# Column convolution of a convolution and recurrence block: two blocks of 256 tokens in one instruction

## The chip, the cores and the metric

The kernel runs on one core of one Trainium2 chip. The metric is device time in microseconds for one execution. The engines are TensorE (PE; its weight loads are PEld), VectorE (DVE), ScalarE (ACT), GpSimd (POOL) and the queue of SyncE (SP), which issues transfers.

## The reference

One layer over 4096 latent tokens of 1024 channels, a grid of 64 by 64. One projection of the normalised input gives q, two forget gates, v and a gate for a bidirectional gated recurrence (4 heads of 128), and u with two gates for a convolution of width 31: half of its 512 channels along the rows of the grid, half along its columns. Both branches are normalised, gated, put side by side, projected, added to the input and normalised again.

```python
def conformer_conv_latent(u, rows, conv_w_l, conv_b_l, ln_g_l, ln_b_l):
    grid = u.reshape(bsz, rows, GRID_W, ch)
    k_row = conv_w_l[:, :half].reshape(1, CONV_WIDTH, 1, half)
    k_col = conv_w_l[:, half:].reshape(CONV_WIDTH, 1, 1, half)
    y = jnp.concatenate([depthwise_conv2d(grid[..., :half], k_row),
                         depthwise_conv2d(grid[..., half:], k_col)], axis=-1).reshape(bsz, t, ch)
    return conv_tail(y, conv_b_l, ln_g_l, ln_b_l)      # silu(layernorm(y + conv_b))

def merge_branches(o_hgrn, g_a, conv_y, g_b, hgrn_norm_g_l, w_out_l):
    branch_a = head_rmsnorm(o_hgrn, hgrn_norm_g_l) * jax.nn.silu(g_a)
    branch_b = conv_y * jax.nn.silu(g_b)
    return jnp.concatenate([branch_a, branch_b], axis=-1) @ w_out_l

...
a_lat = rmsnorm(h_lat, norm_g[l]) * (1.0 + sc_l) + sh_l
q_l, zf_l, zb_l, v_l, ga_l, u_l, ug_l, gb_l = jnp.split(a_lat @ w_in[l], SPLITS, axis=-1)
o_l, _, _ = hgrn2_bidir(q_l, v_l, zf_l, zb_l, lb_f, lb_b, s_f, s_b)
y_l = conformer_conv_latent(u_l * jax.nn.sigmoid(ug_l), rows, conv_w[l], ...)
h_lat = h_lat + gt_l * merge_branches(o_l, ga_l, y_l, gb_l, hgrn_norm_g[l], w_out[l])
return rmsnorm(h_lat, final_norm_g)
```

The columns' convolution reads, for each token, the tokens 15 grid rows above it to 15 below, 960 tokens either way.

## The kernel before

Tokens are worked on in 16 blocks b of 256 (TB), and in 32 groups g of 128, two to a block. A **first sweep** goes through the blocks upward: projections, the recurrence hgrn(b) forward (with sums for the backward one kept for later), and the convolution along rows (`row_conv`, VectorE, L711), whose result goes to memory (`yrd`) for all blocks but the last. Block 15's stays in a tile `yc15`. A block's keys for the recurrence are split by ScalarE (L560) and VectorE (L561, `K`), turned by a transfer that SP issues (L562), and used by TensorE (`pu`, L578); `po` (L822, L823) is the recurrence's output, taken up into `op` (L828), `qu` (L837) is the last block's copy of a sum.

While the last blocks run, the gated inputs of the columns' convolution of all blocks come back from memory into one tile `gu_all` (L1001, 15 transfers on SP).

The **second sweep** goes through the groups downward, 31 to 0, since it needs the backward state `s_b`. Its parts are Python generators, which `merge` interleaves by their counts of steps:

- `gates(b)`: 48 matmuls of 512 columns (`ps_ga`, L1071) and 96 of 256 (`ps_gb`, L1083) for a block, each taken up by ScalarE (L1075, L1092). It is the work with which TensorE can fill time.
- `col_conv(b)`: VectorE alone. Two instructions for the middle tap (L1105), then 60 for the others (L1116), each over one half of the channels on 128 partitions and the 256 tokens of the block, fewer where the grid's edge cuts them.
- `group_front(g)`: `pi` (TensorE, L1144), `op` (VectorE adds, L1145), `s_b` (L1147), four transposes `ps_c` of the convolution's result (L1152), `bn_stats` (L1155) and what follows it, the seed of a reciprocal root (VectorE, L78), its three rounds of four small POOL instructions (L87 to L90), and ScalarE's `yn` (L1171) and `ops` (L1173).
- `group_back(g)`: four transposes `ps_d` of `yn` (L1188), silu, the gates, the split into two halves `yh`, `yl`, and the transposes `ps_o` (L1203).
- `group_out(g)`: 48 matmuls `py` (L1220), the residual `xr` (L1224), a last norm with POOL's L84 and L85, and the transfer out (L1235).

In one turn of the loop at L1252, `group_out(g)`, `group_back(g - 1)`, `group_front(g - 2)`, half of a convolution and half of a block's gates are merged; the convolution of a block runs some two groups ahead of its use. Tiles come from pools: `e1` holds named places ("A", "xt", "gu0" to "gu2") for both sweeps, `m1` only for the first, `m2` only for the second, so a tile in `m2` must wait until the first sweep has let `m1` go. A scheduler then sets one fixed order for each engine; every engine works through its own in order, and stands still where the next instruction's input is not there.

Of the kernel before, what the change touches and what calls it, by code (L numbers as in the profile page):

```python
# [98 lines left out]
def hymba_block(  # L99
# [97 lines left out]
    with ExitStack() as s1:  # L197
# [855 lines left out]
    with ExitStack() as s2:  # L1053
# [8 lines left out]
        def gates(b, d):  # L1062
# [14 lines left out]
            for ct in (0, 2):  # L1077
# [169 lines left out]
        fng = e1.tile([P, D], F32, tag="A", name="fng")  # L1247
        fg1 = final_norm_g.rearrange("(o n) -> o n", o=1)
        nc.sync.dma_start(fng, bass.AP(fg1.tensor, fg1.offset, [[0, P], [1, D]]))

        gate = conv = None
        for g in range(NG + 1, -1, -1):  # L1252
            gens = []
            if g < NG:
                gens.append((N_OUT, group_out(g, ds[g // 2])))
            if 0 < g <= NG:
                gens.append((N_BACK, group_back(g - 1, ds[(g - 1) // 2])))
            if g > 1:
                if g > 2:
                    load_group2(g - 3, ds[(g - 3) // 2])  # L1260
                gens.append((N_FRONT, group_front(g - 2, ds[(g - 2) // 2])))
            b = g // 2 - 2
            if g % 2:
                if 0 <= b:
                    conv = col_conv(b, ds[b])
                    gens.append((31, part(conv, 31)))
                if gate:
                    gens.append((7, gate))
                    gate = None
            else:  # L1270
                if conv:
                    gens.append((31, conv))
                    conv = None
                if 0 < b < NB - 2:
                    load_block(b - 1, ds[b - 1])
                if 0 <= b < NB - 2:
                    gate = gates(b, ds[b])
                    gens.append((7, part(gate, 7)))
                elif gate:
                    gens.append((7, gate))  # L1280
                    gate = None
            if g == NG + 1:
                gate = gates(NB - 2, ds[NB - 2])
                gens.append((7, part(gate, 7)))
# [29 lines left out]
```

## Time and profile before

| | |
|---|---|
| median of 3 runs | 2177.08 us (2176.64 to 2177.74) |
| the profiled execution | 2179.47 us, of which the span is 2177.7 us |
| busy share of the span | PE 94%, PEld 70%, DVE 81%, ACT 46%, POOL 17% |
| instructions | PE 22339, DVE 4283, ACT 2326, POOL 886 |
| the column convolution's taps, L1116 | 828 into `ycs`, 345.3 us, 471 ns each in the mean |

The profiled execution is read as one timeline. Busy time is the time in which an engine has work in it; where VectorE's instructions follow one another without a gap, their times overlap a little, so the distance from start to start is what one costs. A number in brackets behind a row of the timeline is the idle time ahead of it and what ended it. "issue" is time for which no releaser is seen.

### The profile page before, as it was taken

The numbers are of one execution on the slowest core, as the hardware profiler recorded it, in microseconds if no ns is written. First come the engines' busy times: TensorE is split into PE (matmuls) and PEld (weight loads), VectorE is DVE, ScalarE is ACT, GpSimd is POOL, SyncE is SP. The second block draws the span as 40 slices with busy tenths as digits, with TensorE's granted clock in tenths as the row PEclk, the third lists the DMA queues.
The fourth block names the chain that finished last, engine by engine and source line by source line (L and its number), as shares of the span: only waits on it lengthen the run. The fifth ranks groups of instructions, "written<-read, shape, count | busy, mean of one in ns | idle before, by whom it ended". The sixth has DMA issues, their size and how long they took to land. (4 is left out here: it accounts for less than half of the span.)

```text
span 2177.7 us, 54464 instructions
## 1 busy us (share of the span) xinstructions
PE 2056.2 (94%) x22339; PEld 1517.2 (70%) x22339; DVE 1757.6 (81%) x4283; ACT 1006.0 (46%) x2326; POOL 371.6 (17%) x886
## 2 busy tenths in 40 slices
PE   6999999999998998999999999989999999999998
PEld 3777778778777887777788888655555555565664
DVE  5988877977975978978887975969999888888744
ACT  4944546445446445455445434433343333343343
POOL 1110101101101101101101100013433333333222
PEclk8999999999999999999999999989999999999999
DMA  9436155335235254253333225443332222333221
GB/s 363 136 90 161 60 151 161 69 113 130 71 113 144 74 145 138 63 161 114 74 108 63 52 55 156 152 155 102 107 107 93 97 98 92 120 120 115 97 78 59
DMA packets 222082, 247.96 MB, mean 114 GB/s; under 512 B 143652, under 2 KB 151672, under 8 KB 217864
## 3 DMA queue, kind: packets, MB, share of 16 engines
q1 hardware_dynamic: 221288, 240.19, 37.8%
q8 instruction: 175, 2.87, 0.6%
q0 software_dynamic: 544, 4.29, 0.5%
q14 instruction: 75, 0.61, 0.1%
HBM read 138.52 MB, written 72.36 MB: 97 GB/s over the span
## 5 line engine op out<-in xcount | busy, mean ns | idle before, releaser
L289 PEld LDWEIGHTS <-w 128*128 128x128 f16 x4704 | 456.2, 98 | 61.8 <-issue 3.6
L711 DVE SCALAR_TENSOR_TENSOR yr<-gu,convw,yr 128x224 f32<-128x224 f32 (+2 forms) x900 | 357.9, 445 | 0.0
L1116 DVE SCALAR_TENSOR_TENSOR ycs<-gu_all,convw,ycs 128x256 f32<-128x256 f32 (+2 forms) x828 | 345.3, 471 | 0.0
L289 PEld LDWEIGHTS <-pair 128*128 128x128 f16 x3168 | 308.2, 98 | 39.4 <-issue 0.6
L1220 PE MATMUL py<-wo,yh 128*128 128x512 f16 x1024 | 251.4, 381 | 2.9 <-ACT yh L1204 2.9
L289 PE MATMUL ps_z<-aT,pair 128*128 128x256 f16 x1632 | 190.8, 276 | 0.0
L289 PE MATMUL ps_z<-aT,w 128*128 128x256 f16 x1632 | 188.6, 274 | 1.9 <-DVE aT L247 1.4
L1083 PE MATMUL ps_gb<-aT,w 128*128 128x256 f16 x1536 | 187.7, 273 | 0.0
L81 POOL TENSOR_SCALAR xqh<-xssq 128x1 f32<-128x1 f32 x30 | 12.5, 416 | 1022.8 <-DVE xssq L262 1022.8
L300 PE MATMUL pv<-w,aT 128*128 128x512 f16 x816 | 184.4, 379 | 1.3 <-DVE gu L675 1.3
L1071 PE MATMUL ps_ga<-w,aT 128*128 128x512 f16 x768 | 182.1, 382 | 0.0
L289 PE MATMUL ps_u<-aT,w 128*128 128x256 f16 x1536 | 181.3, 274 | 0.2 <-ACT q L657 0.2
L756 ACT COPY km<-X 128x512 f32<-128x512 f32 x160 | 107.9, 675 | 156.1 <-DVE X L764 155.8
L289 PE MATMUL ps_g<-aT,w 128*128 128x256 f16 x1536 | 177.8, 273 | 0.6 <-ACT q L657 0.6
L1220 PEld LDWEIGHTS <-yh 128*128 128x128 f16 x1024 | 100.4, 98 | 108.5 <-ACT yh L1204 4.0
L289 PE MATMUL ps_q<-aT,pair 128*128 128x256 f16 x1536 | 173.3, 273 | 0.0
L1083 PEld LDWEIGHTS <-w 128*128 128x128 f16 x1536 | 150.1, 98 | 31.8
L300 PEld LDWEIGHTS <-aT 128*128 128x128 f16 x816 | 77.4, 98 | 88.2 <-issue 1.5
L1071 PEld LDWEIGHTS <-aT 128*128 128x128 f16 x768 | 75.5, 99 | 81.6 <-issue 2.5
L1220 PE MATMUL py<-wo,yl 128*128 128x512 f16 x512 | 129.6, 379 | 0.0
L1226 ACT ACTIVATE jk<-xr 128x512 bf16<-128x512 f32 x64 | 40.3, 629 | 184.7 <-DVE xr L1224 128.4
L319 ACT ACTIVATE f<-f,lbv,oml 128x128 f32<-128x128 f32 x272 | 112.9, 486 | 0.0
(308 smaller groups left out, 3301.5 us busy)
## 6 DMA issues: line engine op xcount, KB each, us to landing
xt<-in_x_dram SPq DMA_DIRECT2D x32, 512.0 KB, 4.3
xr<-in_x_dram SPq DMA_DIRECT2D x32, 512.0 KB, 3.6
out_dram<-xr SPq DMA_DIRECT2D x31, 512.0 KB, 2.6
aTd<-aT SPq DMA_DIRECT2D x14, 1024.0 KB, 5.1
aT<-aTd SPq DMA_DIRECT2D x14, 1024.0 KB, 5.2
wst<-in_w_in_dram SPq DMA_DIRECT2D x16, 512.0 KB, 4.3
qb<-qbd SPq DMA_DIRECT2D x32, 256.0 KB, 2.7
ub<-ubd SPq DMA_DIRECT2D x32, 256.0 KB, 2.7
```

The costliest lines, as they stand in the source:

```text
L81: eng.tensor_scalar(h, v, -0.5, 0.0, ALU.mult, ALU.add)
L289: nc.tensor.matmul(ps[:, j, :], w[:, wi, k, (ct + j) * P : (ct + j + 1) * P], aT[:, ai, k, :], start=n == 0, stop=n == 23)
L300: nc.tensor.matmul(pv, aT[:, ai, k, i * P : (i + 1) * P], W[G_V][:, wi, k, :], start=n == 0, stop=n == 23)
L319: nc.scalar.activation(fa, fa, AF.Identity, scale=oml[:, d, ct + j : ct + j + 1], bias=lbv[:, d, ct + j : ct + j + 1])
L711: nc.vector.scalar_tensor_tensor(ar[i][:, :, lo:hi], gr[i][:, :, lo + dl : hi + dl], convw[:, i, j : j + 1], ar[i][:, :, lo:hi], ALU.mult, ...
L756: nc.scalar.copy(fap(km, 0, kd), fap(Xs[gi], 0, ks))
L1071: nc.tensor.matmul(ps, aT[:, ai, k, i * P : (i + 1) * P], Wa[:, wi, k, :], start=n == 0, stop=n == 23)
L1083: nc.tensor.matmul(ps[:, j, :], Wb[:, wi, k, (ct + j) * P : (ct + j + 1) * P], aT[:, ai, k, :], start=n == 0, stop=n == 23)
L1116: nc.vector.scalar_tensor_tensor(ya, gu_all[:, i, (lo + dl) * GW : (hi + dl) * GW], convw[:, 2 + i, j : j + 1], ya, ALU.mult, ALU.add)
L1220: nc.tensor.matmul(py, y[:, k // 4, k % 4, :], W2["o", nh][:, wi, k, :], start=n == 0, stop=n == 23)
L1226: nc.scalar.activation(junk, h[:, sl], AF.Square, accum_out=hs[:, nh : nh + 1])
```

## The change

The columns' convolution is done for two blocks at once (a pair p of blocks 2p and 2p + 1), over 512 tokens in one instruction, for pairs 6 to 0. The last two blocks, 15 and 14, which the second sweep needs first, are still done one by one, 256 tokens wide, but now both into one tile `ycl` in the place "A" of `e1`. Row results no longer share a tile with column results: block 15's lie in `yr15` (place "gu2"), those of the others are fetched by a new `load_rows` into `yrow`. So the gates of even blocks use the places "gu0" and "gu1" instead of "gu2" and "gu1". The last norm's factors `fng` move from "A" to "xt". In a turn of the loop 15 or 16 steps of a pair's convolution stand where 31 of a block's stood, over four turns instead of two; pair 6 begins in the first turn, beside block 14's 61 steps.

```diff
@@ row_conv @@
-                late["yc"] = e1.tile([P, 4, TB], F32, tag="A", name="yc15")
-            acc = late["yc"][:, 0:2, :] if b == NB - 1 else m1.tile([P, 2, TB], F32, tag="yr", name="yr")
+                late["yc"] = e1.tile([P, 2, TB], F32, tag="gu2", name="yr15")
+            acc = late["yc"] if b == NB - 1 else m1.tile([P, 2, TB], F32, tag="yr", name="yr")
@@ gates @@
-                    gb = e1.tile([P, 2, TB], F32, tag=f"gu{2 - ct // 2}", name="gb")
+                    gb = e1.tile([P, 2, TB], F32, tag=f"gu{ct // 2}", name="gb")
@@ col_conv @@
-        def col_conv(b, d):
-            yc = late["yc"] if b == NB - 1 else m2.tile([P, 4, TB], F32, tag="ycs", name="ycs", bufs=2)
-            d["yc"] = yc
+        def load_rows(b, d):
+            d["yr"] = late["yc"] if b == NB - 1 else m2.tile([P, 2, TB], F32, tag="yrow", name="yrow", bufs=2)
             if b < NB - 1:
-                nc.sync.dma_start(yc[:, 0:2, :], yrd[b])
-            r0 = b * TB // GW
-            nr = TB // GW
+                nc.sync.dma_start(d["yr"], yrd[b])
+
+        def col_conv(p, half=None):
+
+            if half is None:
+                yc = m2.tile([P, 2, 2 * TB], F32, tag="ycs", name="ycs", bufs=2)
+            elif half:
+                late["ycl"] = yc = e1.tile([P, 2, 2 * TB], F32, tag="A", name="ycl")
+            else:
+                yc = late["ycl"]
...
+            r0 = 2 * p * TB // GW
+            nr = 2 * TB // GW
+            if half is not None:
+                r0, nr = r0 + half * TB // GW, TB // GW
+                yc = ds[2 * p + half]["yc"]
...
@@ second sweep @@
-        merge((N_COL, col_conv(NB - 1, ds[NB - 1])), (N_GATE, gates(NB - 1, ds[NB - 1])))
+        merge((N_COL, col_conv(NB // 2 - 1, 1)), (N_GATE, gates(NB - 1, ds[NB - 1])))
...
+        gate = gates(NB - 2, ds[NB - 2])
+        first = col_conv(NB // 2 - 1, 0)
         for g in range(NG + 1, -1, -1):
...
+            if g >= NG:
+                gens += [(N_GATE // 2, part(gate, N_GATE // 2) if g > NG else gate), (31, part(first, 31 if g > NG else 30))]
+                if g == NG:
+                    gate = None
+            if g % 4 == 1 and g >= 9:
+                conv = col_conv((g - 9) // 4)
+            if conv:
+                n = 15 if (g - 9) % 4 != 2 else 16
+                gens.append((n, part(conv, n)))
+                if g % 4 == 2:
+                    conv = None
```

Line numbers shift: the taps L1116 become L1129, `op` L1145 becomes L1158, `bn_stats` L1155 becomes L1168, `ps_c` L1152 becomes L1165, `ps_d` L1188 becomes L1201.

**Order, first place.** VectorE at the end of the first sweep, from the last step of block 14's keys on (`K`, L561; `s_f`, L583, is the forward state, `FL` L539 belongs to block 15). Before:

```order
L774 TENSOR_TENSOR X_18578<-X_18578,FL_18580 128x8x64
L561 SCALAR_TENSOR_TENSOR K_19356<-X_18577,K_19356 128x512
L561 SCALAR_TENSOR_TENSOR K_19360<-X_18577,K_19360 128x512
L561 SCALAR_TENSOR_TENSOR K_19375<-X_18578,K_19375 128x512
L561 SCALAR_TENSOR_TENSOR K_19379<-X_18578,K_19379 128x512
L583 SCALAR_TENSOR_TENSOR s_f_270<-s_f_270,FL_18579,pu_19391 128x128 x4
L539 TENSOR_TENSOR FL_19493<-f_18739 128x2x256
```

After:

```order
L774 TENSOR_TENSOR X_18578<-X_18578,FL_18580 128x8x64
L1118 TENSOR_SCALAR ycl_20310<-gu_all_19490,convw_83,vec_82 128x256 x2
L561 SCALAR_TENSOR_TENSOR K_19356<-X_18577,K_19356 128x512
L561 SCALAR_TENSOR_TENSOR K_19360<-X_18577,K_19360 128x512
L1129 SCALAR_TENSOR_TENSOR ycl_20310<-gu_all_19490,convw_83,ycl_20310 128x256 x12
L561 SCALAR_TENSOR_TENSOR K_19375<-X_18578,K_19375 128x512
L1129 SCALAR_TENSOR_TENSOR ycl_20310<-gu_all_19490,convw_83,ycl_20310 128x256 x2
L561 SCALAR_TENSOR_TENSOR K_19379<-X_18578,K_19379 128x512
L1129 SCALAR_TENSOR_TENSOR ycl_20310<-gu_all_19490,convw_83,ycl_20310 128x256 x2
```

The taps of block 14 (`ycl`, `x12` for twelve in a row) now stand between the four `K`, where nothing stood.

**Order, second place.** ScalarE in hgrn of block 15 (`K` L560, `qu` and `ub` L837, `v16` L568, `op` L828, `gb` the gates' results). Before:

```order
L1075 ACTIVATE ga_20529<-ps_ga_20584,es_91 128x512
L560 ACTIVATE K_20174<-X_19492 128x512
L560 ACTIVATE K_20178<-X_19492 128x512
L837 ACTIVATE qu_20182<-pu_20191,es_91 128x512
L568 ACTIVATE v16_20209<-v_19893 128x512
L1092 ACTIVATE gb_20764<-ps_gb_20648,es_91 128x512
L828 ACTIVATE op_20243<-po_20230,es_91 128x512
L1092 ACTIVATE gb_20847<-ps_gb_20766,es_91 128x512
```

After:

```order
L560 ACTIVATE K_20174<-X_19492 128x512
L560 ACTIVATE K_20178<-X_19492 128x512
L1092 ACTIVATE gb_20882<-ps_gb_20793,es_91 128x512
L837 ACTIVATE qu_20182<-pu_20191,es_91 128x512
L568 ACTIVATE v16_20209<-v_19893 128x512
L1092 ACTIVATE gb_20791<-ps_gb_20664,es_91 128x512
L828 ACTIVATE op_20243<-po_20230,es_91 128x512
L837 ACTIVATE ub_20262<-pu_20249,es_91 128x512
```

One `gb` went ahead of `qu`, and the other, which lies in the place "gu0", stands ahead of `op` with nothing between.

**Order, third place.** VectorE around `bn_stats` of group 27, the first group of block 13 (`yn`, `ops`, `yl` are the groups' own steps, `xr` and `hv` those of the last norm). Before, with the taps into one tile:

```order
L1147 SCALAR_TENSOR_TENSOR s_b_84<-s_b_84,fb_all_85,ub_21041 128x128
L1116 SCALAR_TENSOR_TENSOR ycs_21321<-gu_all_19490,convw_83,ycs_21321 128x256
L1195 TENSOR_TENSOR yn_20999<-yn_20999,gb_20847 128x256
L1116 SCALAR_TENSOR_TENSOR ycs_21321<-gu_all_19490,convw_83,ycs_21321 128x256
L1192 TENSOR_TENSOR ops_20849<-ops_20849,ga_20529 128x512
L1155 BN_STATS bs_21373<-ps_c_21368 128x6
L1116 SCALAR_TENSOR_TENSOR ycs_21321<-gu_all_19490,convw_83,ycs_21321 128x256
L1205 SCALAR_TENSOR_TENSOR yl_21142<-ps_o_21214,ky_251,yh_21141 128x512
```

After, with the taps into two tiles, of pair 6 (`ycs_20540`) and of pair 5 (`ycs_21335`):

```order
L1129 SCALAR_TENSOR_TENSOR ycs_21335<-gu_all_19490,convw_83,ycs_21335 128x512
L1247 SCALAR_TENSOR_TENSOR xr_21072<-xr_21072,hr_21537,fng_20687 128x1024
L1129 SCALAR_TENSOR_TENSOR ycs_21335<-gu_all_19490,convw_83,ycs_21335 128x512
L1129 SCALAR_TENSOR_TENSOR ycs_20540<-gu_all_19490,convw_83,ycs_20540 128x448 x2
L1129 SCALAR_TENSOR_TENSOR ycs_21335<-gu_all_19490,convw_83,ycs_21335 128x512 x2
L1237 SCALAR_TENSOR_TENSOR xr_21313<-py_21679,kinv_254,xr_21313 128x512
L1129 SCALAR_TENSOR_TENSOR ycs_20540<-gu_all_19490,convw_83,ycs_20540 128x384 x2
L1129 SCALAR_TENSOR_TENSOR ycs_21335<-gu_all_19490,convw_83,ycs_21335 128x512 x2
L1168 BN_STATS bs_21382<-ps_c_21377 128x6
L1129 SCALAR_TENSOR_TENSOR ycs_20540<-gu_all_19490,convw_83,ycs_20540 128x320
```

Narrow taps at the edge of pair 6 and wide ones of pair 5 alternate ahead of `bn_stats`.

## Rows read from the trace of the kernel before

**Rows 1.** Table of stretches: start:end, length, then busy time of each engine, PEclk the granted clock.

```profile
core 0: us, PE busy (x) PEld busy (x) DVE busy (x) ACT busy (x) POOL busy (x), PEclk, DMA share, GB/s
1340.00:1420.00 80.00, 77.67 (x1005) 54.85 (x1003) 70.94 (x174) 30.63 (x58) 1.17 (x2) 1.00 0.60 178
1420.00:1440.00 20.00, 19.69 (x168) 14.79 (x167) 5.19 (x14) 4.77 (x8) 0.00 (x0) 1.00 0.32 93
1440.00:1460.00 20.00, 12.07 (x70) 8.69 (x68) 18.39 (x54) 8.42 (x28) 4.21 (x15) 0.73 0.82 289
1560.00:1860.00 300.00, 283.72 (x1694) 171.01 (x1692) 261.98 (x676) 107.64 (x305) 104.62 (x253) 0.99 0.32 106
1860.00:2170.00 310.00, 308.92 (x1846) 185.06 (x1846) 218.69 (x553) 121.73 (x339) 88.05 (x274) 1.00 0.28 94
```

**Rows 2.** TensorE's own timeline: start, length, engine, line, operation, shapes, count, idle before.

```profile
1380.37 1.89 PE L1071 MATMUL ps_ga<-w,aT 128*128 128x512 f16 x8
...
1544.38 0.66 PE L1188 MATMUL ps_d<-ident,yn 128*128 128x128 f32 x4 [1.21 <-ACT yn L1171]
...
1755.31 1.46 PE L1220 MATMUL py<-wo,yh 128*128 128x512 f16 x6
...
2167.32 1.89 PE L1220 MATMUL py<-wo,yl 128*128 128x512 f16 x8
```

**Rows 3.** TensorE's waits (total us, times, longest us): 1360 to 1560, then 1560 to 2178.

```profile
PE ps_d L1188 <- ACT yn L1171: 8.2, 3, 3.8
PE pi L1144 <- DMA qb<-qbd: 2.3, 1, 2.3
...
PE ps_d L1188 <- ACT yn L1171: 14.4, 7, 3.0
```

**Rows 4.** Timeline at group 21: TensorE, VectorE, POOL, ScalarE.

```profile
1741.85 0.60 PE L1152 MATMUL ps_c<-ident,ycs 128*128 128x128 f32 x4
...
1759.75 0.94 PE L1188 MATMUL ps_d<-ident,yn 128*128 128x128 f32 x4 [2.98 <-ACT yn L1171]
...
1747.23 0.69 DVE L1155 BATCH_NORM_STATS2 bs<-ps_c 128x6 f32<-128x512 f32 x1
...
1752.90 0.17 DVE L78 TENSOR_SCALAR or<-osq 128x5 int32<-128x5 int32 x1
1752.97 3.64 DVE L1116 SCALAR_TENSOR_TENSOR ycs<-gu_all,convw,ycs 128x256 f32<-128x256 f32 x9
1756.53 0.74 DVE L1205 SCALAR_TENSOR_TENSOR yl<-ps_o,ky,yh 128x512 f16<-128x512 f32 x1
1757.19 0.87 DVE L1116 SCALAR_TENSOR_TENSOR ycs<-gu_all,convw,ycs 128x256 f32<-128x256 f32 x2
...
1753.99 0.31 POOL L89 TENSOR_SCALAR ort<-ort 128x5 f32<-128x5 f32 x1
1754.38 0.31 POOL L90 TENSOR_TENSOR or<-or,ort 128x5 f32<-128x5 f32 x1
...
1757.03 0.20 POOL L89 TENSOR_SCALAR ort<-ort 128x5 f32<-128x5 f32 x1
1757.31 0.41 POOL L90 TENSOR_TENSOR or<-or,ort 128x5 f32<-128x5 f32 x1
...
1758.94 0.76 ACT L1171 ACTIVATE yn<-ps_c,lnm,or 128x512 f32<-128x512 f32 x1
```

**Rows 5.** Timeline at the first sweep's end: VectorE, then SP's queue.

```profile
1348.68 0.69 DVE L561 SCALAR_TENSOR_TENSOR K<-X,K 128x512 f16<-128x512 f32 x1 [7.63 <-ACT K L560]
...
1414.45 0.69 DVE L561 SCALAR_TENSOR_TENSOR K<-X,K 128x512 f16<-128x512 f32 x1
...
1443.10 0.68 DVE L1145 TENSOR_TENSOR op<-pi,op 128x512 f32<-128x512 f32 x1
...
1340.91 0.52 SPq L1001 DMA_DIRECT2D gu_all<-gud  x1
1341.54 5.24 SPq L562 DMA_TRANSPOSE X<-K  x2
```

More of the change, by code (lines that the diff above doesn't have):

```diff
@@ L1095, in hymba_block @@
         N_GATE = 14
-        def col_conv(b, d):
-            yc = late["yc"] if b == NB - 1 else m2.tile([P, 4, TB], F32, tag="ycs", name="ycs", bufs=2)
-            d["yc"] = yc
+        def load_rows(b, d):
+            d["yr"] = late["yc"] if b == NB - 1 else m2.tile([P, 2, TB], F32, tag="yrow", name="yrow", bufs=2)
             if b < NB - 1:
-                nc.sync.dma_start(yc[:, 0:2, :], yrd[b])
-            r0 = b * TB // GW
-            nr = TB // GW
+                nc.sync.dma_start(d["yr"], yrd[b])
[6 more added lines that the diff above has]
+                yc = late["ycl"]
+            for b in (2 * p, 2 * p + 1):
+                ds[b]["yc"] = yc[:, :, (b % 2) * TB : (b % 2 + 1) * TB]
+            r0 = 2 * p * TB // GW
[3 more added lines that the diff above has]
+                yc = ds[2 * p + half]["yc"]
             for i in range(2):
-                nc.vector.tensor_scalar(yc[:, 2 + i, :], gu_all[:, i, b * TB : (b + 1) * TB], convw[:, 2 + i, HALF : HALF + 1],
+                nc.vector.tensor_scalar(yc[:, i, :], gu_all[:, i, r0 * GW : (r0 + nr) * GW], convw[:, 2 + i, HALF : HALF + 1],
                                         vec[:, R_CB + 2 + i : R_CB + 3 + i], ALU.mult, ALU.add)
@@ L1114, in col_conv @@
                     if lo < hi:
-                        ya = yc[:, 2 + i, (lo - r0) * GW : (hi - r0) * GW]
+                        ya = yc[:, i, (lo - r0) * GW : (hi - r0) * GW]
                         nc.vector.scalar_tensor_tensor(ya, gu_all[:, i, (lo + dl) * GW : (hi + dl) * GW], convw[:, 2 + i, j : j + 1],
@@ L1138, in group_front @@
             op, ub, qb = d[g]
-            yc = d["yc"]
+            yr, yc = d["yr"], d["yc"]
             tk = slice(gi * P, (gi + 1) * P)
@@ L1151, in group_front @@
             for j in range(4):
-                nc.tensor.transpose(ps[:, j * P : (j + 1) * P], yc[:, j, tk], ident)
+                nc.tensor.transpose(ps[:, j * P : (j + 1) * P], (yr if j < 2 else yc)[:, j % 2, tk], ident)
             bs = sm.tile([P, 6], F32, tag="bs", name="bs")
@@ L1242, in hymba_block @@
             ds[b]["aT"] = aTs[b]
-        merge((N_COL, col_conv(NB - 1, ds[NB - 1])), (N_GATE, gates(NB - 1, ds[NB - 1])))
+        merge((N_COL, col_conv(NB // 2 - 1, 1)), (N_GATE, gates(NB - 1, ds[NB - 1])))
+        load_rows(NB - 1, ds[NB - 1])
+        load_rows(NB - 2, ds[NB - 2])
         for g in (NG - 1, NG - 2):
@@ L1246, in hymba_block @@
         load_block(NB - 3, ds[NB - 3])
[L1247 to L1251, printed above, removed]
+        conv = None
+        gate = gates(NB - 2, ds[NB - 2])
+        first = col_conv(NB // 2 - 1, 0)
         for g in range(NG + 1, -1, -1):
             gens = []
+            if g == NG:
+                fng = e1.tile([P, D], F32, tag="xt", name="fng", bufs=2)
+                fg1 = final_norm_g.rearrange("(o n) -> o n", o=1)
+                nc.sync.dma_start(fng, bass.AP(fg1.tensor, fg1.offset, [[0, P], [1, D]]))
             if g < NG:
@@ L1261, in hymba_block @@
                 gens.append((N_FRONT, group_front(g - 2, ds[(g - 2) // 2])))
+            if g >= NG:
+                gens += [(N_GATE // 2, part(gate, N_GATE // 2) if g > NG else gate), (31, part(first, 31 if g > NG else 30))]
+                if g == NG:
+                    gate = None
[5 more added lines that the diff above has]
+                if g % 4 == 2:
+                    conv = None
             b = g // 2 - 2
             if g % 2:
[L1264 to L1268, printed above, removed]
-                    gate = None
[L1270 to L1274, printed above, removed]
-                    load_block(b - 1, ds[b - 1])
[L1276 to L1284, printed above, removed]
+                if b >= 0:
+                    load_rows(b, ds[b])
+                if gate and g < NG:
+                    gens.append((N_GATE // 2, gate))
+                    gate = None
+            elif 0 <= b < NB - 2:
+                if b > 0:
+                    load_block(b - 1, ds[b - 1])
+                gate = gates(b, ds[b])
+                gens.append((N_GATE // 2, part(gate, N_GATE // 2)))
             merge(*gens)
```

## The prediction

> **What bounds the kernel now.** I read the page's shares and slices first, then a table of stretches, TensorE's waits, VectorE's groups, and last the engines side by side at one stall. The change acts only from the end of the first sweep on, some 840 us. From 1860 to 2170 us TensorE is busy 308.9 of 310 us; from 1560 to 1860 it is busy 283.7 of 300 us, and in 1440 to 1460 us only 12.1 of 20 us, at a granted clock of 0.73 [rows 1]. The reader is to see that only these holes can be won: the work itself, 743.4 us from the first gate matmul at 1380.37 us to the last `py`, is the same in both kernels, and the last `py` starts at about 2168.8 us [rows 2]. (The price of a 512-column matmul is 0.216 us, from six in 1.46 us and eight in 1.89 us [rows 2]; 256 columns are half.) So TensorE loses 2168.8 - 1380.4 - 743.4 = 45.0 us in all. At `ps_d` of group 26, at 1544.38 us, 140.6 us of work were done, so 23.4 us were lost by then: the **start-up part**. The other 21.6 us are lost until 1860 us: the **steady part**.
>
> Who makes the holes? TensorE's waits name `ps_d` behind `yn` first: 8.2 us of 1360 to 1560 us and 14.4 us behind that [rows 3]. ScalarE is not the cause, it is only last in a chain. At group 21 [rows 4] `ps_c` is done at 1742.45 us, but VectorE comes to `bn_stats` only at 1747.23 and to the seed L78 at 1752.90, since convolution taps stand ahead; then twelve small POOL steps, `yn` at 1758.94, and `ps_d` at 1759.75 after 2.98 us of standing still. From L78 to `ps_d` are 6.9 us. VectorE, busy 262.0 of 300 us there [rows 1], sets the steady holes through its queue.
>
> **The wide taps.** Nine taps over 256 columns take 3.64 us and two 0.87, so one follows the other after (3.64 - 0.87) / 7 = 0.396 us [rows 4]. No tap over 512 columns is in this trace; nearest is the same instruction over 512 columns with one input in PSUM, L1205, after which the next starts 0.66 us later [rows 4]. Bounds for a wide tap: 0.66 us, and 2 x 0.396 = 0.79 if width saved nothing. I take 0.66, the same form and size. The straight line through the two is 0.128 us and 1.04 ns a column. The sweep's convolution goes from 896 instructions to 502, 394 fewer, of which each saved 0.128 us: 49 us of VectorE time, about 7 us for each pair of blocks. Nothing of it is TensorE's; it counts only where a hole is.
>
> [...]
>
> **Steady part.** Before, the four groups of two blocks carry 45, 17, 45 and 17 taps of 0.396 us, after 29, 21, 12 and 0 of 0.66 us. Other work of VectorE is about 7.9 us a group, TensorE's is 23 us (both from their orders, each instruction at such a start-to-start price). Before, a heavy group needs 17.8 + 7.9 = 25.7 us against 23, and stalls about 3 us; those are the holes at groups 23, 21, 19, 17, 15 and 13. After, the heaviest needs 19.1 + 7.9 = 27.0 us, but the one ahead of it needs 7.9 and leaves VectorE waiting, and in TensorE's new order `ps_d` of every fourth group stands 3.3 us later. Bounds: 0 left of the 21.6 us, or all of it (nothing shows that only the average counts). I take 2 us left, since in the rows VectorE falls behind only where a heavy group follows one that used up its slack.
>
> **The end of the first sweep.** The changed kernel computes block 14's column taps there, 46 instructions, about 18 us with the two first, in VectorE's order between the `K` of blocks 14 and 15. Before, VectorE is busy 70.9 of 80 us there [rows 1]; one gap of 7.63 us stands ahead of `K` at 1348.68 us [rows 5]. Twelve taps fall into that gap, but they need transfers of `gu_all`, of which SP issues the sixth at 1340.91 us [rows 5], and two more of these issues now go ahead of the transposes on SP; so I let `K` start 2 to 3 us later, and the first `K` of block 15 (1414.45 us [rows 5]) about 7 us later. The chain from there to `op` of group 31 (1443.10 us [rows 5]) is hgrn(15)'s own: transposes, `pu`, `qu`, `v`, `po`. In it TensorE's order has less gate work as filler, and ScalarE's order now has `gb` in `gu0` ahead of `op`, where it must wait for the last row tap that reads `gu0`; together I put 3 us on these. `op` of group 31 comes at 1453, 10 us later; bounds +4 (if the gap takes most of the taps) and +14 (if all but 4 us of the 18 lie on the path).
>
> **Start-up of the second sweep.** Pair 6 must be done over its full width before group 27 is read, and VectorE's order mixes pair 5's taps in as well. Pricing each instruction in VectorE's order from `op` of group 31 on, L78 of groups 30, 27 and 26 comes after 15.2, 73.2 and 85.2 us before, and after 27.7, 107.6 and 112.6 us now. TensorE's work ahead of their `ps_d` is 74.9, 154.3 and 158.3 us now (140.6 for group 26 before). What TensorE must have lost by group 26, if VectorE never stands still, is 1453 + 112.6 + 6.9 - 1380.4 - 158.3 = 33.8 us. The same sum for before gives 1443.1 + 85.2 + 6.9 - 1380.4 - 140.6 = 14.2 against 23.4 measured, so VectorE's own waits (for ACT, POOL, `py`) add 9.2 us. I take 6 for after, since more taps stand ready as filler; bounds 3 and 10.
>
> **POOL beside wide taps.** In [rows 4] POOL's steps follow each other after 0.39 us while 256-column taps run, and after 0.28 us while L1205 runs, which reads one input from PSUM: a step gets through once per tap. If that holds, steps beside wide taps come every 0.66 us. [...] By [rows 4], the chain from L78 to the end of the last POOL step, 4.8 us before, takes up to 6.7 us where ten wide taps stand behind L78 (0.66 us for 0.40 in the steps beside them). At group 27 that adds 1.6 us, and its sum, 1453 + 107.6 + 6.9 - 1380.4 - 154.3 = 32.8 us, becomes 34.4; with 6 us of waits the start-up part is about 41 us where before it was 23.4: **17 us lost**.
>
> The sum: 41 + 2 = 43 us against 45, 2 us less. The tail after the last `py`, 8.9 us, has no convolution and stays. Other edits (row results in their own tiles, fetched as before; `fng` in another tile a little later) I cost at nothing: their transfers are issued groups ahead of their readers; without that cover the nearest row is the 2.3 us for which `pi` waits for `qb` [rows 3]. The profiled execution took 2179.47 us, 2.4 above the median of 2177.08; 2177.5 by its measure is **2175 us** as a median.
>
> **The rivals.** (a) *Forecast*: start-up loss and steady gain nearly cancel, 2170 to 2181, centre 2175. Chance 0.50. (b) *The start-up is hardly later*: block 14's taps fit into VectorE's gaps (5.2 of 20 us busy in 1420 to 1440 us [rows 1] speaks for room, though those gaps lie behind `K`). `op` +2 to +7 us and waits of 3 to 4 us make 29 to 36 us lost, with 2 steady 31 to 38: 2163 to 2170. Chance 0.28. (c) *Slower by the start-up*: `op` of group 31 +14 us and 10 us of waits, so 33.8 + 4 + 10 + 1.6 = 49.4, and 2 steady: 51 us, 2183. It decides from `op` later than about 1456 us. For it speaks that VectorE is nearly full from 1350 to 1418, against it the 15 us free behind. Chance 0.12. (d) *POOL takes VectorE's place*: the chain behind L78 grows by 2 us and the heavy group is 27.0 - 24.5 = 2.5 us above TensorE's work between the two `ps_d`; if the slack of the light group doesn't carry over, up to 4.5 us in each of some four groups, 18 us after 41: 59 us, 2191; at half of that 2182. Chance 0.07. (e) *Width saves nothing* (0.79 us a tap): pair 6's taps ahead of group 27 cost some 7 us more and the heavy groups 23 + 7.9 = 31 us: above 2185. Chance 0.03, since L1205's row speaks against it.
>
> **How the numbers follow.** A measurement here tells about 0.2%, 4.4 us, from no change: below 2172.7 is faster, above 2181.5 slower. (a) splits 0.10, 0.38, 0.02; (b) is all faster; (c) 0.02 same and 0.10 slower; (d) and (e) slower. Together 0.38 faster, 0.40 same, 0.22 slower. The range reaches to the ends of (b) and (c), with 2 us for their own terms above, and leaves out what lies beyond them of (b), (d) and (e): 2163 to 2185.
>
> **What would show it.** Right: conv taps over 512 columns starting 0.66 us apart; `op` of group 31 near 1453; `ps_d` of group 26 near 1380 + 158 + 41 = 1580 us; next to no wait of `ps_d` from 1620 us on; POOL's steps 0.66 us apart beside taps; the period of a block 46 us from then on. Wrong: `op` of group 31 before 1449 (then (b)), after 1456 (c), or waits of `ps_d` on `yn` above 6 us behind 1620 us (d).

## The result: 0.8% slower, and the profile after

The changed kernel takes 2193.8 us (median of 4 runs, 2192.36 to 2196.29) against 2176.87 us of the kernel before (4 runs): ratio 1.0078, 95% interval 1.0063 to 1.0093, some 17 us **slower**. The forecast was 2175, the range 2163 to 2185. The later comparisons ran on other chips, where the kernel before takes 2168.15, 2176.66 and 2176.08 us in the median and its single executions spread by 15 to 20 us; every ratio below stands against runs of the kernel before on the same chip.

The page of after, its first rows (busy time of each engine, share of the span, instructions):

```profile
span 2190.6 us, 54071 instructions
## 1 busy us (share of the span) xinstructions
PE 2062.7 (94%) x22339; PEld 1522.2 (69%) x22339; DVE 1709.8 (78%) x3889; ACT 1006.8 (46%) x2326; POOL 386.7 (18%) x886
```

VectorE is busy 1709.8 us instead of 1757.6: the work went down as planned. The span grew by 12.9 us all the same. The same table of stretches as [rows 1]:

```profile
core 0: us, PE busy (x) PEld busy (x) DVE busy (x) ACT busy (x) POOL busy (x), PEclk, DMA share, GB/s
1440.00:1460.00 20.00, 8.83 (x63) 6.62 (x61) 14.58 (x30) 4.72 (x17) 4.63 (x13) 0.77 0.63 224
1460.00:1480.00 20.00, 16.98 (x68) 9.24 (x68) 19.18 (x40) 6.53 (x22) 5.32 (x13) 0.72 0.24 79
1560.00:1860.00 300.00, 283.70 (x1682) 172.07 (x1681) 233.49 (x467) 117.65 (x335) 112.53 (x280) 0.98 0.30 103
1860.00:2170.00 310.00, 306.48 (x1842) 185.19 (x1841) 180.37 (x391) 121.30 (x336) 88.61 (x267) 0.99 0.29 96
```

From 1560 to 1860 us VectorE has 233.5 us of work where it had 262.0, and TensorE is still busy 283.7 us, as it was. From 1440 to 1480 us TensorE works 25.8 of 40 us, at a mean granted clock of 0.77 and 0.72 in the two halves. Before it worked 32.1 us there, at 0.73 [rows 1] and, in the second half, 0.92:

```profile
1460.00:1480.00 20.00, 20.00 (x115) 11.68 (x113) 18.81 (x46) 10.97 (x34) 3.66 (x12) 0.92 0.13 41
```

TensorE's waits (total, times, longest), first up to 1580 us, then behind it, to be set beside [rows 3]:

```profile
engine line waited for: us in total, times, longest us
PE ps_d L1201 <- ACT yn L1184: 10.5, 3, 4.3
PE pi L1157 <- DVE ycs L1129: 7.8, 1, 7.8
...
PE ps_d L1201 <- ACT yn L1184: 15.3, 8, 3.1
```

The eight stand at groups 23, 22, 19, 18, 15, 14, 11 and 7, the longest (2.9, 2.9 and 3.1 us) at 19, 15 and 11. Before, the seven of [rows 3] stood at groups 25, 22, 21, 19, 17, 15 and 13, so not quite where the prediction has them.

I call **lost** at a group the start of its first `ps_d`, less the first gate matmul, less the work in TensorE's order between them, as in the prediction. (A 256-column matmul costs 0.109 us, since in before eight of `ps_gb` take 1.04 us and sixteen 1.91.) For after, the first gate matmul starts at 1378.51 us, `ps_d` of group 26 at 1574.77 with 158.3 us of work ahead, `ps_d` of group 0 at 2165.83 with 727.2: lost are 38.0 us by group 26 and 60.1 us by group 0. Before it was 23.4 and 45.3. So the start-up part lost 14.6 us more, and the steady part is 22.1 us as against 21.9: **nothing of the steady part came back**. The first gate matmul came 1.9 us earlier, so the span grew by 14.8 - 1.9 = 12.9 us.

Group 15 of after, as [rows 4] shows one of before (TensorE, VectorE, POOL, ScalarE; `lnm` is POOL's last step ahead of `yn`):

```profile
1800.14 0.38 PE L1165 MATMUL ps_c<-ident,ycs 128*128 128x128 f32 x2
...
1820.98 0.66 PE L1201 MATMUL ps_d<-ident,yn 128*128 128x128 f32 x4 [2.87 <-ACT yn L1184]
...
1804.76 0.69 DVE L1168 BATCH_NORM_STATS2 bs<-ps_c 128x6 f32<-128x512 f32 x1
...
1812.03 0.17 DVE L78 TENSOR_SCALAR or<-osq 128x5 int32<-128x5 int32 x1
1812.11 1.41 DVE L1129 SCALAR_TENSOR_TENSOR ycs<-gu_all,convw,ycs 128x512 f32<-128x512 f32 x2
1813.43 0.74 DVE L1218 SCALAR_TENSOR_TENSOR yl<-ps_o,ky,yh 128x512 f16<-128x512 f32 x1
1814.09 3.39 DVE L1129 SCALAR_TENSOR_TENSOR ycs<-gu_all,convw,ycs 128x512 f32<-128x512 f32 x5
...
1813.66 0.20 POOL L89 TENSOR_SCALAR ort<-ort 128x5 f32<-128x5 f32 x1
1813.94 0.20 POOL L90 TENSOR_TENSOR or<-or,ort 128x5 f32<-128x5 f32 x1
...
1814.96 0.59 POOL L88 TENSOR_TENSOR ort<-ort,osq 128x5 f32<-128x5 f32 x1
1815.64 0.57 POOL L89 TENSOR_SCALAR ort<-ort 128x5 f32<-128x5 f32 x1
1816.30 0.58 POOL L90 TENSOR_TENSOR or<-or,ort 128x5 f32<-128x5 f32 x1
1816.95 0.58 POOL L87 TENSOR_TENSOR ort<-or 128x5 f32<-128x5 f32 x1
...
1818.49 0.26 POOL L1181 TENSOR_SCALAR lnm<-ba,or 128x1 f32<-128x1 f32 x1
...
1818.41 1.28 ACT L1186 ACTIVATE ops<-ops,or 128x128 f32<-128x128 f32 x4 [9.35 <-POOL or L90]
1819.60 0.67 ACT L1092 ACTIVATE gb<-ps_gb,es 128x512 f32<-128x512 f32 x1
1820.17 0.76 ACT L1184 ACTIVATE yn<-ps_c,lnm,or 128x512 f32<-128x512 f32 x1
```

Wide taps start 0.66 us apart ((3.39 - 1.41) / 3). Beside them POOL's steps start 0.68, 0.66 and 0.65 us apart; beside L1218, which reads PSUM, 0.28 us. TensorE stands still for 2.87 us at `ps_d`. The steps of the chain, from the end of `ps_c` on, in us (each the difference of two starts or ends in the timelines):

| group 15 | to `bn_stats` | to L78 | to the end of POOL's last step | to `yn` | to `ps_d` | sum | of it TensorE waits |
|---|---|---|---|---|---|---|---|
| before | 4.2 | 5.7 | 5.3 | 0.7 | 0.8 | 16.7 | 2.4 |
| after | 4.2 | 7.3 | 6.7 | 1.4 | 0.8 | 20.5 | 2.9 |
| halves (256 columns, below) | 2.2 | 8.0 | 5.3 | 0.8 | 2.1 | 18.3 | 0 |
| each tap twice (below) | 2.2 | 8.0 | 5.3 | 0.7 | 2.0 | 18.3 | 0 |
| two rounds (below) | 3.4 | 7.3 | 5.2 | 0.8 | 0.8 | 17.5 | 1.7 |
| every second tap (below) | 4.2 | 6.6 | 3.9 | 0.9 | 0.8 | 16.4 | 0.1 |
| after, taps held back (below) | 3.8 | 1.1 | 6.3 | 0.8 | 2.7 | 14.8 | 0 |

TensorE's order has 17.6 us of work between `ps_c` and `ps_d` here (20.5 - 2.9), and had 14.3 before. The new order does put `ps_d` 3.3 us later, as the prediction read; the chain grew by 3.7: 1.6 up to L78, 1.4 in POOL's steps, and 0.7 ahead of `yn`, since ScalarE's order now has a `gb` (L1092) between `ops` and `yn`, which stood behind `yn` before.

The wait is the idle time ahead of `ps_d` in TensorE's timeline. The sum less the wait is TensorE's work in between, and the order that is made anew for each kernel sets it too (15.8 us with two rounds, 18.3 in halves): each experiment shows its edit together with a new order. ([Rows 4] and the prediction call their group 21. Counted from the first `ps_d`, of group 31, it is group 17, with 4.8, 5.7, 5.3, 0.7 and 0.8 us; the reading does not hang on the number.)

### The profile page after: what moved, and what is told of

Its sections match the earlier page's. It is cut to its first block, busy times and chain, and to the rows that moved or that the text cites. A ratio compares the mean times of both kernels' runs of the same rounds, so it can differ in the third digit from the quotient of the medians.

```text
span 2190.6 us, 54071 instructions
## 1 busy us (share of the span) xinstructions
PE 2062.7 (94%) x22339; PEld 1522.2 (69%) x22339; DVE 1709.8 (78%) x3889; ACT 1006.8 (46%) x2326; POOL 386.7 (18%) x886
## 3 DMA queue, kind: packets, MB, share of 16 engines
q8 instruction: 175, 2.87, 0.6%
## 5 line engine op out<-in xcount | busy, mean ns | idle before, releaser
L711 DVE SCALAR_TENSOR_TENSOR yr<-gu,convw,yr 128x196 f32<-128x196 f32 (+14 forms) x960 | 382.5, 447 | 0.0
L1129 DVE SCALAR_TENSOR_TENSOR ycs<-gu_all,convw,ycs 128x512 f32<-128x512 f32 (+6 forms) x404 | 272.6, 716 | 0.0
L81 POOL TENSOR_SCALAR xqh<-xssq 128x1 f32<-128x1 f32 x30 | 12.1, 404 | 1023.3 <-DVE xssq L262 1023.3
```

Source lines behind the costliest of these rows:

```text
L81: eng.tensor_scalar(h, v, -0.5, 0.0, ALU.mult, ALU.add)
```

## Experiments

Lost time in all kernels, in us, with the starts from which it is worked out:

| kernel | first gate matmul | `ps_d` 26, work ahead | lost by 26 | `ps_d` 0, work ahead | lost by 0 | behind 26 | ratio to before (95%) |
|---|---|---|---|---|---|---|---|
| before | 1380.37 | 1544.38, 140.6 | 23.4 | 2152.85, 727.2 | 45.3 | 21.9 | 1 |
| after | 1378.51 | 1574.77, 158.3 | 38.0 | 2165.83, 727.2 | 60.1 | 22.1 | 1.0078 (1.0063 to 1.0093) |
| after, again | 1380.05 | 1575.93, 158.3 | 37.6 | 2171.02, 727.2 | 63.8 | 26.2 | 1.0077 (1.0049 to 1.0106) |
| halves | 1376.47 | 1579.90, 156.5 | 46.9 | 2153.55, 727.2 | 49.9 | 3.0 | 1.0043 (1.0028 to 1.0058) |
| each tap twice | 1377.53 | 1586.45, 163.0 | 45.9 | 2162.01, 727.2 | 57.3 | 11.4 | 1.0049 (1.0025 to 1.0074) |
| every second tap | 1379.74 | 1555.09, 143.3 | 32.0 | 2139.61, 727.2 | 32.7 | 0.7 | 0.9974 (0.9960 to 0.9988) |
| after, taps held back | 1373.48 | 1545.17, 139.9 | 31.7 | 2148.59, 727.2 | 47.9 | 16.2 | 1.0047 (1.0032 to 1.0062) |
| before, taps held back | 1374.43 | 1541.27, 142.0 | 24.8 | 2141.89, 727.2 | 40.3 | 15.5 | 1.0015 (1.0001 to 1.0030) |
| pair 6 in halves | 1376.65 | 1583.83, 164.3 | 42.9 | 2170.98, 727.2 | 67.1 | 24.2 | 1.0088 (1.0059 to 1.0117) |
| block by block in own tiles | 1377.68 | 1544.23, 137.0 | 29.6 | 2153.92, 727.2 | 49.0 | 19.4 | 0.9972 (0.9948 to 0.9996) |
| the same, again | 1375.17 | 1540.10, 137.0 | 28.0 | 2146.65, 727.2 | 44.3 | 16.3 | 1.0015 (0.9996 to 1.0034) |
| after, two rounds | 1377.31 | 1572.04, 158.6 | 36.1 | 2150.13, 726.1 | 46.7 | 10.6 | 1.0005 (0.9988 to 1.0022) |
| before, two rounds | 1381.34 | 1548.89, 143.2 | 24.4 | 2141.32, 726.1 | 33.9 | 9.5 | 0.9945 (0.9923 to 0.9967) |
| own tiles, two rounds | 1379.46 | 1542.54, 137.4 | 25.7 | 2135.16, 726.1 | 29.6 | 3.9 | 0.9937 (0.9916 to 0.9957) |

The work is rounded, so a difference can be off by 0.1. A lost time is one profiled execution; after and after again differ by 4 us behind group 26, so differences below 5 us there say nothing. The kernel before was profiled on the first chip alone. What a kernel costs is therefore read from the ratios, and the lost times only tell where it goes.

### What keeps the steady part

**Halves.**

```diff
...
+            elif True:
+                for h in (1, 0):
+                    yield from taps(ds[2 * p + h]["yc"], r0 + h * TB // GW, TB // GW)
...
-                n = 15 if (g - 9) % 4 != 2 else 16
+                n = 31 if (g - 9) % 4 > 1 else 30
```

Here `taps` is the loop over the taps of `col_conv`; `h` is 1 for the odd block, which is needed first.

> The changed kernel, but each pair's convolution in two halves of 256 columns, the odd block (needed first) ahead of the even one; everything else as changed. Two theories of why the steady part still loses 22 us (ps_d of group 26 to the end). Queue theory: taps stand in clumps ahead of a group's short chain on VectorE (48, 37, 26, 8 taps of 0.396 us in four groups here, 29, 21, 6, 4 of 0.66 us in the changed kernel), width does not matter: steady part 22 to 28 us, POOL's steps back to 0.39 us apart. POOL theory: the stalls remain because POOL's steps wait 0.66 us behind wide taps: steady part falls to about 10 us. Start-up part (36 us in the changed kernel): 31 to 36, since only the odd half must be done before group 27. Time: queue 2190 to 2200, POOL 2175 to 2182.

Measured 1.0043. Behind group 26 3.0 us are lost, not 22 to 28: the queue theory falls as I had put it, although the clumps are as long in time as those of after, and VectorE has 48 us more work. Group 15 of this kernel (VectorE, POOL, TensorE):

```profile
1811.16 0.16 DVE L78 TENSOR_SCALAR or<-osq 128x5 int32<-128x5 int32 x1
...
1812.69 3.64 DVE L1135 SCALAR_TENSOR_TENSOR ycs<-gu_all,convw,ycs 128x256 f32<-128x256 f32 x9
...
1814.87 0.32 POOL L88 TENSOR_TENSOR ort<-ort,osq 128x5 f32<-128x5 f32 x1
1815.28 0.31 POOL L89 TENSOR_SCALAR ort<-ort 128x5 f32<-128x5 f32 x1
1815.67 0.31 POOL L90 TENSOR_TENSOR or<-or,ort 128x5 f32<-128x5 f32 x1
...
1819.26 0.60 PE L1207 MATMUL ps_d<-ident,yn 128*128 128x128 f32 x4
```

POOL's steps stand 0.41 and 0.39 us apart again, and `ps_d` has no wait. Behind 1580 us, TensorE's waits for `yn` come to 2.5 us in 3 times:

```profile
PE ps_d L1207 <- ACT yn L1190: 2.5, 3, 1.5
```

But the start-up part rose to 46.9 us where I had expected 31 to 36, against both theories: in VectorE's order 107 taps now stand between the L78 of group 28 and that of group 27, and block 13 has 52 in all, so at least 55 of them are for blocks needed later.

**Each tap twice**, so that the order of blocks stays that of after.

```diff
+                        mid = max(lo, hi - 4) if half is None else lo
+                        for l, h in ((mid, hi), (lo, mid)):
+                            if l < h:
+                                ya = yc[:, i, (l - r0) * GW : (h - r0) * GW]
...
```

> The changed kernel with each wide tap issued as two instructions of 256 columns directly behind one another; turns, tiles and run-ahead are the changed kernel's, VectorE has about 48 us more work. POOL theory (a POOL step gets through once per tap, so wide taps lengthen the chain behind L78): steps back to 0.39 us apart, L78 to lnm from 6.7 to 5.3 us, and of the 18 to 26 us behind group 26 at most 8 stay. Work theory (VectorE's load sets the stalls): 22 to 35 us behind group 26. Start-up loss by group 26: 40 to 50 us in both, for the additional work ahead of group 27. Time: POOL theory 0.2 to 0.6% above the kernel before, work theory 1.0% or more.

1.0049, within what the POOL theory gave for the time, and 11.4 us behind group 26: between the two forecasts, nearer to POOL's. Group 15 has the chain of the halves (POOL's part 5.3 us) and no wait; at group 19, though, POOL's part took 8.4 us and TensorE stood still for 3.4 us. One POOL step lies over nine narrow taps there instead of one:

```profile
1719.56 3.57 POOL L90 TENSOR_TENSOR or<-or,ort 128x5 f32<-128x5 f32 x1
```

Both runs with narrow taps lose less behind group 26 than after, with more work on VectorE: width itself costs there.

**Every second tap** of pairs 5 to 0 left out.

```diff
-                    if lo < hi:
+                    if lo < hi and (half is not None or p > 5 or dl % 2):
```

> The changed kernel with every second tap of pairs 5 to 0 left out (the output lacks them); still 512 columns wide. Queue theory: clumps of half the size, 10 + 7.9 us against 23 of TensorE, so the steady part falls from 22 to 0 to 4 us. POOL theory: POOL's steps still run beside wide taps at 0.66 us, so 6 to 12 us stay. Start-up part 32 to 36. Time: queue 2170 to 2176, POOL 2178 to 2186.

0.7 us behind group 26, as the queue theory had it. So the load does matter: at group 15 no tap was left behind L78, POOL's part took 3.9 us, and the chain fell to 16.4 us. This run can't part the theories as I had meant it to, since where taps are few they don't stand beside POOL.

**Taps held back**, in after and in before.

```diff
+                z = m2.tile([P, 1], F32, tag="z", name="z", bufs=2)
+                nc.vector.tensor_scalar(z, late["sq"][:, NH : NH + 1], 0.0, None, ALU.mult)
+                late["cw"] = m2.tile([P, 4, TAPS], F32, tag="cw", name="cw", bufs=2)
+                nc.vector.tensor_scalar(late["cw"], convw, z, None, ALU.add)
...
-                        ... convw[:, 2 + i, j : j + 1], ...
+                        ... cw[:, 2 + i, j : j + 1], ...
```

> The changed kernel with the taps held back: in each turn of the loop the tap weights are copied by a small VectorE instruction that reads the last front's variance (times zero), and the turn's taps read the copy. VectorE's order then has 14 to 16 wide taps in every group instead of 29, 21, 6, 4; the work is the same but for two small instructions a turn. Queue theory: 10.2 + 7.9 us against 23, the steady part falls from 22 us to 0 to 4: 2170 to 2177 with a start-up part of 32 to 36. POOL theory: every group now has wide taps behind its L78 and POOL's steps 0.66 us apart, so the steady part stays at 15 us or more: 2185 or above.

> The kernel before (256 columns, block by block) with the taps held back in the same way: 30 taps in every group instead of 45 and 15 from group 17 on, but 60, 6, 54, 19 above it. Queue theory: 30 x 0.396 + 7.9 = 19.8 us against 23, so from group 17 on no stalls: of the 21.6 us of the steady part 8 to 14 stay (groups 25 to 19): 2165 to 2172. POOL theory: no wide taps here, so nothing changes by it: 2175 to 2179.

After with even taps: 1.0047. From group 21 on, where the taps are even, lost time grows from 43.8 to 47.9 us, 4.1 us, where after grows from 42.2 to 60.1; 12.1 us go between groups 26 and 21, where L78 still follows `bn_stats` after 3.4 to 8.7 us. POOL's part is 6.3 to 6.7 us from group 21 to 13; it does no harm since L78 follows `bn_stats` after 1.1 to 1.9 us. So the wide tap's price in POOL only counts where the taps also stand ahead of L78. Before with even taps: 1.0015, no gain, though the queue theory promised one. (Its lost times are 5 us below those of before in all, but they are of another chip, and no gain shows in the ratio.) From 1660 us on, TensorE's waits there are

```profile
PE py L1222 <- ACT yh L1206: 6.7, 5, 2.0
PE ps_d L1190 <- ACT yn L1173: 3.4, 3, 2.0
```

`py` behind `yh` comes in place of `ps_d` behind `yn`: taps that no longer stand between `bn_stats` and L78 (1.1 us at group 15, 5.7 in before) seem to stand ahead of another step of the group; that is read from this wait alone.

**Two rounds** instead of three in the root, four POOL steps fewer.

```diff
-    for _ in range(3):
+    for _ in range(2 if tag == "or" else 3):
```

> The changed kernel with two rounds instead of three in the root of the fronts, so four POOL steps fewer between L78 and yn (a slightly coarser root). If POOL's steps beside wide taps are part of what holds ps_d, each stall behind group 26 shrinks by 1.6 to 2.6 us: of the 22 us 4 to 10 stay, 10 to 18 us below the changed kernel. If something else ends as late (ScalarE's order, yh, the py matmuls), 18 to 22 us stay.

1.0005 beside 1.0077 of after on the same chip, 16 us (2195.0 to 2179.1 us); 10.6 us behind group 26. TensorE's waits behind 1580 us, 9.1 us in 7 times, none above 1.7:

```profile
PE ps_d L1201 <- ACT yn L1184: 9.1, 7, 1.7
```

At group 15 POOL's part is 5.2 us, 1.5 less, and the wait went from 2.9 to 1.7 (the chain is 3.0 us shorter, and `ps_d` stands 1.8 us earlier in TensorE's order). So POOL's part of the chain lies on the path.

### What costs the start-up

> The changed kernel once more, unaltered, beside the others on the same chip. TensorE's lost time by group 26 about 38 us, and some 22 us behind it; 0.6 to 0.9% above the kernel before.

It came out as in the first comparison: 1.0077.

**Pair 6 in halves**: the edit of the halves, for `p == 6` alone.

> The changed kernel with pair 6 alone in two halves of 256 columns, the odd block first; pairs 5 to 0 stay wide. Two theories of the start-up loss. Width theory: group 27 waits for the whole width of pair 6, so the lost time by group 26 falls from 38 to 25 to 30 us, time 8 to 13 us below the changed kernel. Run-ahead theory: the doubled tile lets VectorE's order run up to four blocks ahead, and whatever is ready is put ahead of group 27, so the lost time stays at 36 to 42 us and the time is that of the changed kernel within 4 us. Behind group 26 both expect 18 to 22 us.

42.9 us by group 26, and 1.0088: that group 27 waits for pair 6's full width is not the cause. VectorE's order still has 79 taps between the L78 of groups 28 and 27 (55 in after, 18 in before).

**Block by block in own tiles.**

```diff
+                yc = None
+                ds[2 * p + half]["yc"] = m2.tile([P, 2, TB], F32, tag="ycs", name="ycs", bufs=2)
...
-            if g % 4 == 1 and g >= 9:
-                conv = col_conv((g - 9) // 4)
+            if g % 2 and 5 <= g < NG:
+                b = g // 2 - 2
+                conv = col_conv(b // 2, b % 2)
```

> The changed kernel, but pairs 6 to 0 block by block again, 256 columns wide, in the turns of the kernel before and each into a tile of its own (two of them), so VectorE's order can run ahead no further than before. Left of the change: block 14's taps in the first sweep, the separate row results and the places of tiles. Run-ahead theory: lost time by group 26 24 to 31 us, behind it about 22 as in the kernel before, so 46 to 53 us in all and 0 to 0.4% above before. Rival (block 14's taps in the first sweep cost the start-up): 36 us or more by group 26, 0.6% or more above before.

> The kernel with block-by-block taps in tiles of their own and block 14's in the first sweep once more, in more rounds, since its first interval (0.9948 to 0.9996) lies close to 1. If the first sweep hides block 14's taps, 0.1 to 0.5% below the kernel before; if that was chance, within 0.15%.

29.6 and 28.0 us by group 26, as run-ahead has it: with two tiles of one block, the order can't go further ahead than before, 44 taps stand ahead of group 27's L78, and 8 to 10 us of the 14.6 are gone. The ratios 0.9972 and 1.0015 lie on either side of 1, and the second is what I had called chance; taken together this kernel can't be told from before. So block 14's taps in the first sweep and the new places cost nothing in time that can be measured, and the loss of the change is width with the doubled tile. The ratios part the two: doubled tile with taps of 256 columns 1.0043 and 1.0049, with taps of 512 columns 1.0078 and 1.0077, although the narrow taps are 48 us more work for VectorE.

What own tiles leave of the start-up loss, 5 to 6 us, is mostly one wait, which after has as well. The end of the first sweep in after (VectorE, TensorE, SP):

```profile
1343.82 4.84 DVE L1129 SCALAR_TENSOR_TENSOR ycl<-gu_all,convw,ycl 128x256 f32<-128x256 f32 x12 [3.23 <-DMA gu_all<-gud]
1348.58 0.69 DVE L561 SCALAR_TENSOR_TENSOR K<-X,K 128x512 f16<-128x512 f32 x1
...
1446.97 0.68 DVE L1158 TENSOR_TENSOR op<-pi,op 128x512 f32<-128x512 f32 x1
...
1453.64 2.04 PE L1157 MATMUL pi<-s_b,qb 128*128 128x128 f32 x8 [7.75 <-DVE ycs L1129]
...
1447.50 0.37 SPq L1143 DMA_DIRECT2D qb<-qbd  x1
```

`K` came at 1348.58 us (1348.68 in [rows 5]), `op` of group 31 only 3.9 us later than before. But `pi` of group 30 then waits 7.75 us, where it waited 2.3 [rows 3]. The row names a tap; in the second run of after, and in that of own tiles (7.10 us), the same wait is put down to the transfer:

```profile
1454.55 2.05 PE L1157 MATMUL pi<-s_b,qb 128*128 128x128 f32 x8 [7.13 <-DMA qb<-qbd]
```

`qb` is issued at 1447.50 us in after and at 1442.57 before, since its tile waits for the first sweep's last, the end of `s_f` at 1447.05 and 1442.54 us; and TensorE's order has no gate matmul left to fill the time, where before 16 of them ran:

```profile
1441.99 3.62 PE L1071 MATMUL ps_ga<-w,aT 128*128 128x512 f16 x16
```

In after this wait is not what decides by group 26. Between `op` of group 31 and L78 of group 27, at 1558.08 us, VectorE stands idle for a `pi` for only 0.2 us, and TensorE waits 4.3 us for that chain at `ps_d` of group 27 (the longest of the three above). With 5 us less at `pi` that wait would be the longer; this is argued, no run shows it.

### A version that is faster than both

> The kernel before with two rounds instead of three in the fronts' root. The steady stalls (21.6 us, some 3 us a heavy group) shrink by 1.6 us each, 8 to 11 us in all: 0.3 to 0.6% below the kernel before. If another wait takes the chain's place: within 0.2%.

> Block-by-block taps in tiles of their own with block 14's in the first sweep (as in the run of that kind), and two rounds instead of three in the fronts' root. The stalls of about 2.5 us a block behind group 24 (the chain from L78 ends last) shrink by the four POOL steps, 1.6 us: of some 20 us 5 to 9 stay; 0.5 to 0.9% below the kernel before. If the chain is not last, as without it: 0.1 to 0.5% below.

0.9945 and 0.9937: both are faster than before, by 12 and 14 us, and so than after, and they don't differ from each other. The root is slightly coarser. Lost time behind group 26 fell to 9.5 and 3.9 us. In the second, TensorE's waits for `yn` behind 1580 us are a single one:

```profile
PE ps_d L1204 <- ACT yn L1187: 2.3, 1, 2.3
```

The gain is that of the shorter root in either, not of the change: with the same root the changed kernel stands at 1.0005.

## Why the prediction was wrong

- **The sum** put 41 us in the start-up part and 2 in the steady part; measured are 38.0 and 22.1. The failed step is the steady part, "I take 2 us left": 22.1, which is the prediction's own upper bound, "all of it".
- It failed in two places. I compared loads of groups (27.0 us against 23, with a light group ahead), but a stall is a matter of one chain against the TensorE work between `ps_c` and `ps_d`: 20.5 us against 17.6 at group 15, with VectorE busy 233.5 of 300 us. The slack of the light group did not carry over: no tap stands between `bn_stats` of groups 17 and 16, and yet at group 15 `bn_stats` comes 4.2 us behind `ps_c`, as before. And I had POOL's price (0.66 us a step, 2 us a chain) in hand and used it in the start-up part alone; in the steady part it went to rival (d), with a chance of 0.07.
- That rival had the mechanism, and its sign came true (15.3 us of waits of `ps_d` on `yn` where above 6 stood for it). That its price, 18 us, is close to the 20.1 us that were missing is in part luck: it has up to 4.5 us in each of four groups, and measured are eight waits of at most 3.1 us, a granted clock of 0.50 behind three of them, and a chain that grew by POOL's 1.4 us, not 2. Halves and two rounds show POOL's part on the path; taps held back show that it takes taps ahead of L78 as well. How the 3.7 us by which the chain grew share the loss is not shown: no run restores ScalarE's order alone.
- **The wide tap**: 0.66 us, as taken. **VectorE's saving** of 49 us (394 times 0.128 is 50): 47.8 us by the page. Both right, and worth nothing here, since a hole depends on which taps stand ahead of L78 and beside POOL in one group, not on VectorE's total.
- **The end of the first sweep**: `op` of group 31 was put at 1453 and came at 1446.97, within the bounds; `K` was not later at all, since twelve taps fit into the gap. By the prediction's own test (below 1449) this pointed to rival (b), with 29 to 36 us by group 26; measured are 38.0.
- **The start-up part**, 17 us more foretold and 14.6 measured, is near by errors that offset each other. `op` came 6.0 us earlier, and VectorE reached L78 of group 27 111.1 us behind it, where the sum had 107.6 and 6 of waits, 2.5 us less. Against that, the first gate matmul came 1.9 us earlier, L78 to `ps_d` of group 27 took 9.8 us instead of 8.5, and 2.9 us were lost between `ps_d` of groups 27 and 26, which the sum had at nothing: behind the wait of 4.3 us the granted clock is 0.50 from 1568 to 1573 us, and eight `pi` take 1.91 us there where the next eight, at 1575.20 us, take 1.06.
- **Run-ahead**: the sum priced the new order as it stood, pair 5's taps ahead of group 27 included, and so had its cost; why they stand there, the doubled tile, is from the kernel with own tiles, not from the prediction.

## What to carry to other kernels

Before widening an instruction so that fewer are needed (here that saves an estimated 0.13 us for each tap less, twice 0.396 us at 256 columns against 0.66 at 512), ask which chain of short steps runs beside it: where the steps of a neighbouring engine start as far apart as these instructions do, as POOL's mostly did here (0.39 us beside 256 columns, 0.66 beside 512), the chain gets longer with the width. Price a stall by the chain that ends last against the work the waiting engine has in between, not by the load of an engine over a period. And a larger tile also lets an order that is made greedily run further ahead; look at what it now puts in front of the first result that is needed.

## What was not expected of the hardware

A POOL instruction on 128 by 5 elements follows the last after 0.28 us beside VectorE's `yl` (L1205, in after L1218), which reads PSUM, and mostly once per tap beside the taps, whose two inputs `gu_all` and `ycs` lie in SBUF: every 0.39 us at 256 columns, every 0.66 us at 512. The mean of L87 went from 288 to 349 ns. First a row of before, then rows of after (busy us, mean ns, then idle time ahead):

```profile
line engine op names shapes xcount | busy us, mean ns | idle before us <-releasers
...
L87 POOL TENSOR_TENSOR ort<-or 128x5 f32<-128x5 f32 x96 | 27.6, 288 | 216.8 <-DVE or L78 193.3 <-ACT yh L1204 17.0 <-DVE hr L78 1.6
```

```profile
L1129 DVE SCALAR_TENSOR_TENSOR ycs<-gu_all,convw,ycs 128x512 f32<-128x512 f32 x362 | 255.4, 744 | 0.0
...
L87 POOL TENSOR_TENSOR ort<-or 128x5 f32<-128x5 f32 x96 | 33.5, 349 | 228.3 <-DVE or L78 206.9 <-ACT jk L1239 16.4
```

But not always: now and then one step lies over a whole run of taps. At group 11 of after one does so over six wide taps, the 3.98 us below, and POOL's part there is 8.6 us; in before, at groups 18, 16 and 14, one lies over ten narrow taps for 3.97 us. What sets these apart no run here shows.

```profile
1911.69 3.98 POOL L90 TENSOR_TENSOR or<-or,ort 128x5 f32<-128x5 f32 x1
```

And the holes of TensorE cost more than their length: of the 22.1 us behind group 26 in after, 15.3 are waits for `yn`. Behind three of these waits (2.9 us until 1723.65, 2.1 until 1845.14, 3.1 until 1920.42 us) the granted clock is 0.50 while TensorE is busy (from 1724 to 1727, 1847 to 1849 and 1922 to 1925 us); behind the other wait of 2.9 us, until 1820.98, it is 1.00 (1821 to 1824). From 1580 to 2170 us its mean is 0.99: 0.01 of 590 us is about 6 us, an estimate, about what is missing. With two rounds, where no wait is above 1.7 us, it is 1.00. After, then after with two rounds:

```profile
1580.00:2170.00 590.00, 574.63 (x3446) 347.42 (x3445) 399.81 (x824) 227.49 (x638) 192.87 (x520) 0.99 0.29 99
1724.00:1727.00 3.00, 3.00 (x10) 1.40 (x9) 3.00 (x8) 1.02 (x5) 0.00 (x0) 0.50 0.00 0
1922.00:1925.00 3.00, 3.00 (x9) 1.08 (x8) 3.00 (x8) 2.40 (x10) 0.06 (x1) 0.50 0.34 87
```

```profile
1580.00:2170.00 590.00, 578.46 (x3479) 348.49 (x3476) 405.44 (x839) 228.57 (x640) 165.25 (x414) 1.00 0.30 100
```
